# A two-layer hybrid transformer block: ScalarE's gate operations of the context stream put in one fixed order by function table, and the query multiplied by its sigmoid

## The chip, the core and the metric

The kernel runs on one core of a Trainium2 chip. The core has a matrix engine (TensorE, PE in the profile; PEld is its weight load), a vector engine (VectorE, DVE), an engine for functions of one element (ScalarE, ACT), a general engine (GpSimd, POOL), and a queue engine (SyncE, SP) that issues DMA transfers. The engines run side by side; each takes its own instructions strictly in order and waits on semaphores for the others. ScalarE evaluates exponentials, logarithms, sigmoids and the like from a function table, and an instruction ACT_TABLE_LOAD in its stream changes the table.

The metric is the device time of the core in microseconds (us).

## The reference

Two streams run through the block: a latent of 512 tokens and a context of 256 tokens, each of width 1024, in float32. Layer 0 mixes tokens by two gated linear recurrences (group A and group B, 4 heads each, run forward and backward), layer 1 by windowed attention; each is followed by a feed-forward network. The change lies in layer 0, in group A's features:

```python
qa = split_heads(jax.nn.silu(a_q) * A_KEY ** -0.5, A_HEADS)
for d, z in enumerate((a_zf, a_zb)):
    f = lb[d] + (1.0 - lb[d]) * jax.nn.sigmoid(z)
    a_dirs.append((qa, split_heads(1.0 - f), va, split_heads(jnp.log(f))))
...
bc = jnp.cumsum(gc, axis=3)          # within a chunk
q_dec = qc * jnp.exp(bc)
k_inv = kc * jnp.exp(-bc)
```

So for each direction the gate goes through a sigmoid, a logarithm, a running sum and two exponentials, and the query through a SiLU, `x * sigmoid(x)`. Group B's gate is a log-sigmoid, made from an absolute value, an exponential and a logarithm, followed by a running sum and exponentials. A recurrent state passes from chunk to chunk, and from the context's end to the latent's start; the context's recurrence comes first.

## The kernel before

Activations lie with features on the 128 partitions and tokens along the free dimension. Each float32 weight matrix comes in tiles of 128x1024 from memory (`raw`, four buffers) and is split into a high part, rounded by ScalarE (`whi`, L139), and the rest, subtracted by VectorE (`wlo`, L140), three buffers each. Every product is three matmuls: high by high, high by low, low by high. A projection of 128 output features is 24 matmuls (L188; for the value and gate tiles, where the activations are the stationary operand, L198 to L200).

The program is written with generators. `merge(main, side, ratio)` takes one step of `main` and then `ratio` steps of `side` in turn; the order in which instructions are written is their priority, moved forward by `cfg["pri"]` places for weight loads and conversions and by `cfg["evp"]` for the copies that empty PSUM. From that a planner, which simulates the engines, makes each engine's order: at each moment it places the first ready instruction by priority. `follow(key, ins)` adds an order without a wait: an instruction with the same key on the same engine may not be placed ahead of the one before it.

The stage of the change, for the context (`SC`; a tile holds two heads, 128x512):

- `rec_group_a(SC)` runs twelve projections: four for the backward gate (s = 2), four for the query (s = 0), four for the forward gate (s = 1). The gates leave PSUM through a sigmoid on ScalarE (L707), the query through a copy on VectorE (L711). The weights of the first six have `pri` 0, of the others 200. The buffers in PSUM rotate over two named "mm" and three named "kv". Then come the value projections, `rec_v_group(SC, 0)`.
- After that `merge` runs, at ratio 3.2, a main line of twelve steps (`rec_group_b`: the low-rank projection L776, the gate's second matrix L783, four projections of query and key; `rec_v_group`; `rec_group_g`) with a side line: `gla_a(SC)`, `gla_b_feat(SC)`, `norm_lat0()`.
- `gla_a` takes the backward direction first. Its first four steps hold only gate operations: the query's SiLU (L950), the logarithm (L958, after VectorE's scaling L957), and for each of two tiles 1 - f (L962), the running sum (`scan_gate`, L831), a difference (L967), edge values on GpSimd (L822, L823), two exponentials (L969, L970), the query's product (L971) and the key's (L972). `trans_a` (L850) makes one small exponential for the decay from chunk to chunk. Then, for each pair of chunks, the key is transposed on TensorE and copied by ScalarE (`kT`, L858), scores and key-value products are formed, the state goes through a product on GpSimd (`S`, L995) and a sum on VectorE (`R`, L1001), and the output (`ps_o`) is taken (`ob`, L1012 to L1019). The forward direction follows in the same way.
- `gla_b_feat` makes group B's features (absolute value L1039, exponential L1040, logarithm L1043, exponentials L1062 and L1063, small exponential L1081), and `norm_lat0` loads the latent (eight tiles), squares it, adds the squares on GpSimd (L361) and normalizes it.

In this order the planner puts ScalarE's gate operations wherever they are ready. The latent's recurrence later runs the same functions with `SL` (a tile holds one head), where group B's exponentials already have a key of their own, "gkl".

Of the kernel before, what the change touches and what calls it, by code (L numbers as in the profile page):

```python
# [11 lines left out]
F32 = mybir.dt.float32  # L12
# [33 lines left out]
def block_kernel(ctx, tc, plan, xT, cT, vecs, w2, cst, atm, rope, ada, rec_a, rec_v, rec_g, rec_o, qk_w, v_w, wo_w, ff_in, ff_out, out):  # L46
# [639 lines left out]
    class Feat:  # L686
        pass
# [3 lines left out]
    def proj_one(st, idx, u):  # L691
        hi, lo = wload(rec_a[idx], 1024)
        p_ = psg()[:, : st.nt]
        gemm_a(p_, [(hi, lo, KD)], u[0], u[1], st)
        return p_

    def rec_group_a(st, u):
# [3 lines left out]
        for s in (2, 0, 1):  # L701
            for h in range(4):
                p_ = proj_one(st, h * 3 + s, u)
                with tc.high_priority(offset=cfg["evp"]):
                    d_ = ch(f.q if s == 0 else f.z[s - 1], st, h)
                    if s and st.name in 'cl':
                        nc.scalar.activation(d_, p_, AF.Sigmoid)  # L707
                    elif {'c': 'd', 'l': 'a'}[st.name] == "a":
# [4 lines left out]

    def rec_group_a2(nh, lat, order, n1):


        ts = {}
        for st in (SC, SL):
            f = feats[st.name]
            f.q = [ut([P, st.r, st.nt], name="qA") for _ in range(4 // st.r)]  # L720
            f.z = [[ut([P, st.r, st.nt], name="zA") for _ in range(4 // st.r)] for _ in range(2)]
        def prod(st, w, s, h):
            f = feats[st.name]
            u = uc if st is SC else ul
            p_ = psg()[:, : st.nt]
            gemm_a(p_, w, u[0], u[1], st)
            with tc.high_priority(offset=cfg["evp"]):
                d_ = ch(f.q if s == 0 else f.z[s - 1], st, h)
                if st is SL and 1:
                    nc.scalar.copy(d_, p_)  # L730
                else:
                    nc.vector.tensor_copy(d_, p_)
        held = []
        def go(a, b):
            for i in range(a, b):
                s, h = order[i]
                if i == nh:
                    yield from lat
                    for a_ in held:
                        prod(SL, *a_)  # L740
                        yield
                if i < nh:
                    w = [(hi, lo, 4) for hi, lo in whold(rec_a[h * 3 + s])]
                    held.append((w, s, h))
                else:
                    w = [wload(rec_a[h * 3 + s], 1024) + (KD,)]
                prod(SC, w, s, h)
                if i >= nh:
                    prod(SL, w, s, h)
                yield  # L750

        return go(0, n1), go(n1, len(order))
# [1016 lines left out]
```

## Time and profile before

| | |
|---|---|
| Time, median of 3 runs | 1786.58 us (1786.05 to 1788.2) |
| The profiled execution: time, span | 1783.1 us, 1780.7 us |
| TensorE's mean granted clock | 0.986 |
| Busy share: PE, DVE, ACT, POOL | 97%, 58%, 47%, 16% |
| The stage of the change, in the profile | about 43 to 194 us |

The busy share of an engine is an average over stages with different limits. In a view by stretches, each engine's busy time stands against the length of the stretch, with the granted clock of TensorE. In a view by groups, a row has line, engine, operation, output and inputs, the count, the busy time, and the mean length of one in ns. In a view of waits, a row says which instruction waited, for which engine's output and line, and how long. In a view in order of time, the first column is the start and the second the length in us; what stands in brackets is the idle time before, and what ended it.

### The profile page before, as it was taken

What the parts mean: (1) busy time and instruction counts of PE and PEld (TensorE: products, weight loads), DVE (VectorE), ACT (ScalarE), POOL (GpSimd) and SP (SyncE); (2) the same over time, 40 slices, a digit from 0 to 9 for tenths busy, and PEclk for the clock granted to TensorE, in tenths of its full rate; (3) what the DMA queues carried; (4) which work ended last, traced back from release to release, by engine and by line L of the source; (5) the groups of instructions that cost most, each with busy time, mean ns of one, the idle gap of its engine ahead of it and who ended that gap; (6) DMA issues with size and microseconds to landing.
All of it is one profiled execution on the core that took longest, in us unless ns stands there. A gap on an engine that the chain in (4) does not pass through costs nothing.

```text
span 1780.7 us, 27528 instructions
## 1 busy us (share of the span) xinstructions
PE 1723.4 (97%) x10807; PEld 1478.9 (83%) x10807; DVE 1037.3 (58%) x1741; ACT 828.4 (47%) x1403; POOL 279.4 (16%) x316
## 2 busy tenths in 40 slices
PE   7989999999999999999999999999899999999997
PEld 3977778798899989988888888987587998888886
DVE  3768544565877636898533436778755853322335
ACT  3975756445845545532222225434756642222232
POOL 1141201222240013100000001124443200000003
PEclk9989999999999999999999999999999999999998
DMA  8536556211335554767535324341021433233323
GB/s 309 165 121 208 171 189 206 94 58 48 95 120 146 174 158 148 245 225 253 168 110 185 94 76 139 108 120 60 1 60 36 150 114 102 79 100 107 96 68 114
DMA packets 87825, 232.39 MB, mean 131 GB/s; under 512 B 10096, under 2 KB 18032, under 8 KB 87696
## 3 DMA queue, kind: packets, MB, share of 16 engines
q1 hardware_dynamic: 87696, 230.64, 41.0%
q8 instruction: 84, 1.38, 0.3%
q14 instruction: 45, 0.37, 0.1%
HBM read 225.36 MB, written 2.10 MB: 128 GB/s over the span
## 4 chain that ended last, share of the span: by engine, by line
PE 88%; DVE 5%; ACT 4%; issue 2%; DMA 0%; SPq 0%; POOL 0%; DVEq 0%; ACTq 0%
PE ps_mm L188 35%; PE ps_kv L188 31%; PE ps_o L1495 2%; PE ps_o L231 2%; PE ps_tr L1488 2%; PE ps_mm L198 2%; PE ps_mm L199 2%; PE ps_mm L200 2%; PE ps_mm L266 1%; PE ps_kv L266 1%; PE ps_tr L231 1%; PE ps_kv L1454 1%; PE ps_tr L377 1%; PE ps_kv L231 1%; ACT whi L139 1%
## 5 line engine op out<-in xcount | busy, mean ns | idle before, releaser
L139 ACT CAST whi<-raw 128x1024 fp32r<-128x1024 f32 (+3 forms) x304 | 298.2, 982 | 568.5 <-issue 215.6
L140 DVE TENSOR_TENSOR wlo<-raw,whi 128x1024 fp32r<-128x1024 f32 (+3 forms) x314 | 365.9, 1166 | 332.8 <-ACT whi L139 322.7
L188 PE MATMUL ps_mm<-uh,whi 128*128 128x512 f32 (+1 forms) x808 | 277.0, 343 | 2.9 <-ACT whi L139 2.9
L188 PE MATMUL ps_mm<-uh,wlo 128*128 128x512 f32 (+1 forms) x808 | 275.3, 341 | 0.3 <-DVE wlo L140 0.3
L188 PE MATMUL ps_mm<-ul,whi 128*128 128x512 f32 (+1 forms) x808 | 274.7, 340 | 0.0
L188 PE MATMUL ps_kv<-uh,whi 128*128 128x512 f32 (+1 forms) x744 | 260.6, 350 | 0.0
L188 PE MATMUL ps_kv<-uh,wlo 128*128 128x512 f32 (+1 forms) x744 | 259.5, 349 | 0.4 <-DVE wlo L140 0.4
L188 PE MATMUL ps_kv<-ul,whi 128*128 128x512 f32 (+1 forms) x744 | 259.7, 349 | 0.0
L361 POOL TENSOR_TENSOR acc<-acc,sq 128x256 f32<-128x256 f32 (+1 forms) x71 | 88.8, 1253 | 998.3 <-ACT sq L360 993.6
L188 PEld LDWEIGHTS ps_mm<-uh,whi 128*128 128x128 f32 x808 | 154.8, 192 | 22.4 <-ACT whi L139 4.2
L188 PEld LDWEIGHTS ps_mm<-uh,wlo 128*128 128x128 f32 x808 | 154.7, 191 | 17.9 <-issue 0.9
L188 PEld LDWEIGHTS ps_mm<-ul,whi 128*128 128x128 f32 x808 | 154.7, 192 | 16.0 <-issue 0.3
L188 PEld LDWEIGHTS ps_kv<-uh,whi 128*128 128x128 f32 x744 | 140.8, 189 | 21.9 <-ACT whi L139 3.4
L188 PEld LDWEIGHTS ps_kv<-uh,wlo 128*128 128x128 f32 x744 | 140.7, 189 | 18.8 <-DVE wlo L140 0.6
L188 PEld LDWEIGHTS ps_kv<-ul,whi 128*128 128x128 f32 x744 | 140.8, 189 | 18.0 <-issue 0.2
L198 PE MATMUL ps_mm<-whi,uh 128*128 128x256 f32 x344 | 100.1, 293 | 4.0 <-ACT gate L804 4.0
L199 PE MATMUL ps_mm<-wlo,uh 128*128 128x256 f32 x344 | 98.8, 288 | 5.1 <-DVE wlo L140 5.1
L188 PE MATMUL ps_mm<-hh,wlo 128*128 128x256 f32 (+1 forms) x299 | 99.8, 334 | 0.9 <-DVE wlo L140 0.9
L188 PE MATMUL ps_mm<-hh,whi 128*128 128x256 f32 (+1 forms) x299 | 100.0, 334 | 0.0
L188 PE MATMUL ps_mm<-hl,whi 128*128 128x256 f32 (+1 forms) x299 | 99.6, 333 | 0.0
L200 PE MATMUL ps_mm<-whi,ul 128*128 128x256 f32 x344 | 98.7, 288 | 0.0
L298 DVE SCALAR_TENSOR_TENSOR aacc<-ar,s,aacc 128x512 f32<-128x512 f32 x112 | 81.3, 758 | 27.3 <-DMA ar<-in_ada_dram 26.7
(323 smaller groups left out, 3362.1 us busy)
## 6 DMA issues: line engine op xcount, KB each, us to landing
raw<-in_ff_in_dram SPq DMA_DIRECT2D x138, 512.0 KB, 3.6
ar<-in_ada_dram SPq DMA_DIRECT2D x192, 256.0 KB, 4.3
raw<-in_ff_out_dram SPq DMA_DIRECT2D x52, 512.0 KB, 3.6
raw<-in_rec_a_dram SPq DMA_DIRECT2D x34, 512.0 KB, 4.5
raw<-in_rec_v_dram SPq DMA_DIRECT2D x16, 512.0 KB, 3.7
raw<-in_rec_g_dram SPq DMA_DIRECT2D x16, 512.0 KB, 3.7
raw<-in_rec_o_dram SPq DMA_DIRECT2D x16, 512.0 KB, 3.6
raw<-in_wo_w_dram SPq DMA_DIRECT2D x14, 512.0 KB, 3.6
```

What stands on the lines that cost most here:

```text
L139: behind(nc.scalar.copy(hi[:, :n], raw[:, :n]))
L140: behind((nc.gpsimd if cfg["lo"][q % len(cfg["lo"])] == "p" else nc.vector).tensor_sub(lo[:, :n], raw[:, :n], hi[:, :n].bitcast(F32)))
L188: mm(ps_, a, b, start=(i == 0), stop=(i == len(q) - 1))
L198: mm(ps, ah, hi[:, s], start=(k == 0), stop=False)
L199: mm(ps, ah, lo[:, s], start=False, stop=False)
L200: mm(ps, al, hi[:, s], start=False, stop=(k == KD - 1))
L231: yield lambda *a, **k: follow(key, mm(*a, **k))
L266: mm(r[32 * g : 32 * g + 32, :], s32[:, k, 30 - 2 * i : 62 - 2 * i], raw, start=(i == 0 and k < 4), stop=(i == n - 1 and k >= 4), tile_pos ...
L298: nc.vector.scalar_tensor_tensor(a, raw, s_, a, ALU.mult, ALU.add)
L361: (nc.vector if i else nc.gpsimd).tensor_add(d, d, q)
L1488: nc.tensor.transpose(tr[:, g * 128 : (g + 1) * 128], Ps[g][:, j * 128 : (j + 1) * 128], ident)
L1495: mm(o[64 * i : 64 * i + 64, :256], VT[kt][:, kv * 64 : kv * 64 + 64], t_[:, 256 * i : 256 * i + 256], start=(j == 0), stop=(j == len(ktil ...
```

## The change

The gate part of `gla_a` becomes a function of its own, `gate_a(st, d)`, with the query's product in `query_a(st, d)`; the result is kept in `f.a[d]`. For the context both are called while `rec_group_a` is still being written: the backward gate after four projections, the query's sigmoid and product after eight, the forward gate after twelve, ahead of the value projections. For the latent they are called in `gla_a` as before, with the query's products after all of a direction's gate operations, and one more step of the generator for each direction.

`tables(st)` gives the key "tables" for the context and none for the latent. All of the context's sigmoids, logarithms and exponentials of groups A and B, and the SiLU of its output gates, get that key in `follow`, so ScalarE has to take them in the order in which they are written: four sigmoids, two logarithms, five exponentials (backward); two sigmoids of the query; four sigmoids, two logarithms, five exponentials (forward); then group B's two exponentials, two logarithms, seventeen exponentials; then the output gates. The context's query is no longer put through a SiLU but through a sigmoid into a new tile, `qs`, and VectorE multiplies the two. Of the context's weights now the first eight have `pri` 0. An unused variant of the projections (`rec_group_a2`, and the branch on `SH`) is removed.

```diff
+    def tables(st):
+        return "tables" if st is SC else None
+
+    def silu_q(st):
+        f = feats[st.name]
+        if st is SL:
+            for q in f.q:
+                nc.scalar.activation(q, q, AF.Silu)
+        else:
+            for q in f.q:
+                g = ut([P, st.r, st.nt], name="qs")
+                follow(tables(st), nc.scalar.activation(g, q, AF.Sigmoid))
+                nc.vector.tensor_mul(q, q, g)
...
-                    if s and st.name in 'cl':
-                        nc.scalar.activation(d_, p_, AF.Sigmoid)
+                    if s:
+                        follow(tables(st), nc.scalar.activation(d_, p_, AF.Sigmoid))
...
-        nc.scalar.activation(e, e, AF.Exp)
+        follow(tables(st), nc.scalar.activation(e, e, AF.Exp))
...
+    def gate_a(st, d):
+        f = feats[st.name]
+        n = st.nch
+        nt4 = 4 // st.r
+        qd, kd = [], []
+        DL = base.tile([P, 4, n], F32, name=uid("dl"), tag=f"dlA{st.name}", bufs=2)
+        BM = base.tile([P, 4, n], F32, name=uid("bm"), tag=f"bmA{st.name}", bufs=2)
+        g0 = gi[0]
+        for i in range(nt4):
+            s = f.z[d][i]
+            for r in range(st.r):
+                h = d * 4 + i * st.r + r
+                nc.vector.tensor_scalar(s[:, r, :], s[:, r, :], oml[:, h : h + 1], lb[:, h : h + 1], ALU.mult, ALU.add)
+            follow(tables(st), nc.scalar.activation(b65(gpad[(g0 + i) % NG])[:, :, 1:65], v8(s, st), AF.Ln))
+        yield
+        for i in range(nt4):
+            s = f.z[d][i]
+            nc.vector.tensor_scalar(s, s, -1.0, 1.0, ALU.mult, ALU.add)
+            bx = scan_gate()
+            E = ut([P, st.r, st.nt], name="E")
+            Ei = ut([P, st.r, st.nt], name="Ei")
+            i0, i1 = decay(bx, d, ALLP)
+            nc.vector.tensor_sub(v8(Ei, st), i0, i1)
+            edge(bx, d, ALLP, flat8(DL, st, i), flat8(BM, st, i))
+            follow(tables(st), nc.scalar.activation(E, Ei, AF.Exp))
+            follow(tables(st), nc.scalar.activation(Ei, Ei, AF.Exp, scale=-1.0))
+            nc.vector.tensor_mul(Ei, Ei, s)
+            qd.append(E)
+            kd.append(Ei)
+            yield
+        f.a[d] = (qd, kd, DL, trans_a(st, d, DL, BM))
+
+    def query_a(st, d):
+        f = feats[st.name]
+        for E, q in zip(f.a[d][0], f.q):
+            nc.vector.scalar_tensor_tensor(E, E, 128.0 ** -0.5, q, ALU.mult, ALU.mult)
...
         for d in (1, 0):
...
+            if d not in f.a:
+                if d == 1:
+                    silu_q(st)
                 yield
-            e = trans_a(st, d, DL, BM)
+                yield from gate_a(st, d)
+                query_a(st, d)
+                yield
+            qd, kd, DL, e = f.a[d]
...
     def gk(st):
-        return "gk" + st.name if st.name in 'l' else None
+        return "gk" + st.name if st is SL else tables(st)
...
-            nc.scalar.activation(tl[i], tl[i], AF.Exp, scale=-1.0)
+            follow(tables(st), nc.scalar.activation(tl[i], tl[i], AF.Exp, scale=-1.0))
...
-            nc.scalar.activation(tl[i], tl[i], AF.Ln, bias=1.0)
+            follow(tables(st), nc.scalar.activation(tl[i], tl[i], AF.Ln, bias=1.0))
...
-        nc.scalar.activation(e, e, AF.Exp, scale=1.0 / 16.0)
+        follow(tables(st), nc.scalar.activation(e, e, AF.Exp, scale=1.0 / 16.0))
...
-        ga = rec_group_a(SC, uc)
-        for i in range(6):
-            cfg["pri"] = 0 if i < 4 else 0
-            next(ga)
-        cfg["pri"] = 200
-        drain(ga, rec_v_group(SC, 0, uc))
+    ga = rec_group_a(SC, uc)
+
+    def steps(n):
+        for _ in range(n):
+            next(ga)
+
+    steps(4)
+    drain(gate_a(SC, 1))
+    steps(4)
+    silu_q(SC)
+    query_a(SC, 1)
+    cfg["pri"] = 200
+    steps(4)
+    drain(gate_a(SC, 0))
+    query_a(SC, 0)
+    drain(rec_v_group(SC, 0, uc))
```

More of the change, by code (lines that the diff above doesn't have):

```diff
@@ L686, in block_kernel, with __init__ @@
     class Feat:
-        pass
+        def __init__(self):
+            self.a = {}
     feats = {"l": Feat(), "c": Feat()}
@@ L705, in rec_group_a @@
                     d_ = ch(f.q if s == 0 else f.z[s - 1], st, h)
-                    if s and st.name in 'cl':
-                        nc.scalar.activation(d_, p_, AF.Sigmoid)
-                    elif {'c': 'd', 'l': 'a'}[st.name] == "a":
+                    if s:
+                        follow(tables(st), nc.scalar.activation(d_, p_, AF.Sigmoid))
+                    elif st is SL:
                         nc.scalar.copy(d_, p_)
@@ L712, in rec_group_a @@
                 yield
[L714 to L752, printed above, removed]
     def rec_v_group(st, g, u):
@@ L936, in gla_a @@
         npair = n // 2
-        nt4 = 4 // st.r
         is_l = st is SL
@@ L1199, in block_kernel @@
     cfg["pri"] = 0
-    SH = 0
-    zside = iter(())
-    if SH:
-        order = [(s, h) for s in [2, 0, 1] for h in range(4)]
-        n1 = 8
-        ga, rest = rec_group_a2(3, norm_lat0(), order, n1)
-        drain(seq(ga, rec_v_group(SC, 0, uc)))
-    else:
-        rest = iter(())
-        ga = rec_group_a(SC, uc)
-        for i in range(6):
-            cfg["pri"] = 0 if i < 4 else 0
-            next(ga)
-        cfg["pri"] = 200
-        drain(ga, rec_v_group(SC, 0, uc))
+    ga = rec_group_a(SC, uc)
+    def steps(n):
+        for _ in range(n):
+            next(ga)
+    steps(4)
[8 more added lines that the diff above has]
+    drain(rec_v_group(SC, 0, uc))
     rr["tags"] = ["mm"]
@@ L1217, in block_kernel @@
     rr["tags"] = ['mm']
-    drain(merge(seq(rest, rec_group_b(SC, uc), rec_v_group(SC, 1, uc), rec_group_g(SC, uc)), seq(gla_a(SC), gla_b_feat(SC), norm_lat0()), 3.2))
+    drain(merge(seq(rec_group_b(SC, uc), rec_v_group(SC, 1, uc), rec_group_g(SC, uc)), seq(gla_a(SC), gla_b_feat(SC), norm_lat0()), 3.2))
     engines("la")
@@ L1222, in block_kernel @@
     ycs, yoc, yac = new_u(SC), new_ys(SC), Acc(SC)
-    drain(merge(merge(seq(rec_v_group(SL, 0, ul)) if SH else seq(rec_group_a(SL, ul), rec_v_group(SL, 0, ul)), ada_gen(0, (2, 4, 3, 5), ada0), 1.8),
+    drain(merge(merge(seq(rec_group_a(SL, ul), rec_v_group(SL, 0, ul)), ada_gen(0, (2, 4, 3, 5), ada0), 1.8),
                 seq(gla_b(SC), gate_y(SC, 0, ycs), gate_y(SC, 1, ycs), rec_out(SC, ycs, yoc, yac)), 2.0))
```

32 lines of the change are left out of this document (removed).

## Prediction

> **What bounds the kernel now.** I read the page's first part, then a table of stretches of the context's recurrent stage, then what TensorE waited for there, then ScalarE's groups and its instructions in order of time.
>
> ```profile
> span 1780.7 us, 27528 instructions
> PE 1723.4 (97%) x10807; PEld 1478.9 (83%) x10807; DVE 1037.3 (58%) x1741; ACT 828.4 (47%) x1403; POOL 279.4 (16%) x316
> ```
>
> TensorE (PE) is busy 97% of the span, so ScalarE (ACT) at 47% sets the end only in places where PE is idle or slowed. The stage of the change is one of them. Columns of the next view: stretch, length, busy time of PE, PEld, DVE, ACT and POOL with counts, then PE's granted clock, share and rate of the DMA engines.
>
> ```profile
> 43.00:53.00 10.00, 10.00 (x86) 10.00 (x85) 8.19 (x11) 9.66 (x13) 1.83 (x2) 1.00 0.58 180
> 53.00:68.00 15.00, 14.59 (x122) 14.39 (x121) 11.18 (x16) 14.79 (x19) 2.03 (x5) 1.00 0.49 152
> 68.00:88.00 20.00, 18.34 (x153) 18.14 (x153) 15.59 (x21) 18.93 (x25) 3.29 (x5) 1.00 0.50 156
> 88.00:113.00 25.00, 20.03 (x145) 16.71 (x144) 15.04 (x18) 20.27 (x38) 7.00 (x14) 0.83 0.29 100
> ...
> 130.00:143.00 13.00, 9.26 (x77) 8.38 (x78) 11.92 (x15) 5.00 (x8) 7.70 (x6) 0.96 0.44 129
> 143.00:160.00 17.00, 17.00 (x118) 14.93 (x119) 11.57 (x19) 4.95 (x9) 0.00 (x0) 0.83 0.62 194
> ```
>
> From 43 to 88 us ACT is the fullest engine beside PE (43.4 of 45 us), yet PE loses only 0.41 + 1.66 us: the weights are converted ahead. From 88 to 113 PE loses 4.97 us and its clock falls to 0.83. From 130 to 143 it loses 3.74 us, with ACT busy for 5.0 of 13 us. So a lighter ACT can buy time between 68 and 113 us and hardly behind that. The waits of PE from 43 to 165 us (us in total, times, longest) say for whom:
>
> ```profile
> PE ps_mm L199 <- DVE wlo L140: 2.9, 2, 1.7
> PE ps_kv L231 <- ACT kT L858: 2.9, 1, 2.9
> PE ps_o L231 <- POOL S L995: 1.9, 1, 1.9
> PE ps_kv L198 <- ACT whi L139: 1.7, 1, 1.7
> PE ps_o L231 <- ACT ob L1017: 1.5, 1, 1.5
> ```
>
> Three of the five are on ACT, 1.7 + 2.9 + 1.5 us. ACT's own groups from 43 to 113 us show what fills it (count, then busy us and mean ns):
>
> ```profile
> L707 ACT ACT_TABLE_LOAD x4 | 5.1, 1283 | 0.1
> L958 ACT ACT_TABLE_LOAD x4 | 5.1, 1283 | 0.1
> L969 ACT ACT_TABLE_LOAD x2 | 2.6, 1283 | 0.0
> L950 ACT ACT_TABLE_LOAD x2 | 2.6, 1283 | 0.0
> L850 ACT ACT_TABLE_LOAD x2 | 2.6, 1283 | 0.0
> L1043 ACT ACT_TABLE_LOAD x2 | 2.6, 1283 | 0.0
> L1062 ACT ACT_TABLE_LOAD x1 | 1.3, 1283 | 0.0
> L1081 ACT ACT_TABLE_LOAD x1 | 1.3, 1283 | 0.0
> ```
>
> That is 18 loads of a function table, 18 x 1.283 = 23.1 us. The same engine in order of time (start, length):
>
> ```profile
> 66.40 0.63 ACT L950 ACTIVATE qA<-qA 128x512 f32<-128x512 f32 x1
> ...
> 67.99 1.28 ACT L707 ACT_TABLE_LOAD   x1
> 69.28 0.39 ACT L707 ACTIVATE zA<-ps_kv 128x256 f32<-128x256 f32 x1
> ...
> 96.25 0.63 ACT L1043 ACTIVATE lsg<-lsg 128x512 f32<-128x512 f32 x1
> ...
> 98.29 1.28 ACT L1062 ACT_TABLE_LOAD   x1
> 101.37 0.42 ACT L1062 ACTIVATE exB<-aB 64x256 f32<-64x256 f32 x1 [1.80 <-DVE aB L1052]
> ...
> 102.55 0.59 ACT L858 COPY kT<-ps_tr 128x512 f32<-128x512 f32 x1
> ...
> 107.55 0.56 ACT L1017 COPY ob<-ps_o 64x512 f32<-64x512 f32 x1
> ```
>
> A SiLU (L950) followed by a sigmoid (L707) costs a load, and so does a logarithm (L1043) followed by an exponential (L1062): sigmoid, SiLU, logarithm and exponential need four different tables here. The copy of kT that PE waited 2.9 us for stands behind such a load and behind an exponential that itself waits 1.80 us for VectorE (DVE); the copy of ob stands behind the second logarithm. PE's matmuls after that wait:
>
> ```profile
> 104.53 0.40 PE L188 MATMUL ps_mm<-ul,whi 128*128 128x256 f32 x1
> 104.73 0.41 PE L188 MATMUL ps_mm<-uh,wlo 128*128 128x256 f32 x1
> ...
> 114.46 0.41 PE L188 MATMUL ps_mm<-ul,whi 128*128 128x256 f32 x1
> ...
> 115.08 0.28 PE L188 MATMUL ps_mm<-uh,wlo 128*128 128x256 f32 x1
> 115.20 0.28 PE L188 MATMUL ps_mm<-uh,whi 128*128 128x256 f32 x1
> ```
>
> From 104.5 to 114.5 us they start 0.20 to 0.21 us apart, from 115.1 on 0.12 us: a slow spell follows the gap. It is 10.0 us long, less the 1.5 us wait for ob in it 8.5 us of work, of which (0.21 - 0.12) / 0.21 = 43% is lost, 3.7 us.
>
> **The change part by part.** *Table loads.* With the context's operations in one fixed order ACT runs: sigmoids of the backward gate, logarithms, exponentials; sigmoids of the query and of the forward gate, logarithms, exponentials and with them the first exponentials of the second head group; its logarithms; its exponentials. That is 8 loads in place of 18, since the query's sigmoid shares the gate's table, which its SiLU did not. 10 x 1.283 = 12.8 us leave ACT: 8 loads among the gates and the query (14 before, all but those of L1043, L1062 and L1081; 6 after), which lie before 88 us, and 2 in the second group's features (4 before).
>
> What of it reaches the end? Between 43 and 80 us nothing: PE has at most 0.41 us of idle time there. The 1.66 us at 82 us (weights behind the loads of the forward gate) I count in full, since the forward gate's sigmoids, logarithms and exponentials then need 3 loads, where each of its logarithms and sigmoids could take one of its own. For the stall of 88 to 113 us there are 2.9 + 1.5 + 3.7 = 8.1 us to be had at most and nothing at least. Of the four loads of the second group's features (L1043 twice, L1062, L1081) two stay; the exponential's wait for DVE stays as well. I take half, 4.1 us. Sum: 1.7 + 4.1 = 5.8 us gained.
>
> A rule weighed here: by the Trainium skill, "TensorE: Matmul & The Clock Gate", Part 1, PE's clock falls to half for a whole window of some 3.4 us, which runs freely, once PE idles in it. The doubled spacing agrees with the half; the spell's length here is three such windows. By that rule the 3.7 us would be gained whole or not at all, so that the sum would be 1.7 + 2.2 + 3.7 = 7.6 or 3.9 us, about the same middle.
>
> A second one bears on the size: "ScalarE: Activation LUTs", What ACT_TABLE_LOAD costs, gives 2.66 us for a switch with its drain. The rows show 1.29 us from the load's start to the next instruction's (67.99 to 69.28). By the page 26.6 us would leave ACT; the row decides.
>
> *The query.* Two SiLUs of 0.63 us become two sigmoids of the same shape, for which the trace has no row from SBUF; from PSUM a sigmoid of half that width takes 0.39 us, so between 0.6 and 0.8 us, no change. Two multiplications are added on DVE.
>
> ```profile
> L972 DVE TENSOR_TENSOR Ei<-Ei,zA x12: 677/692/1528, 54.8 to 385.9; 128x512 f32<-128x512 f32 x12
> 130.01 5.79 DVE L1065 TENSOR_TENSOR EiB<-exiB,qkB 64x256 f32<-64x256 f32 x4
> 137.57 1.71 DVE L1065 TENSOR_TENSOR EiB<-exiB,qkB 64x256 f32<-64x256 f32 x4
> 129.50 6.02 POOL L361 TENSOR_TENSOR acc<-acc,sq 128x512 f32<-128x512 f32 x4
> ```
>
> By L972 they cost 2 x 0.69 = 1.4 us. They lie at about 63 to 67 us, where PE works from weights converted ahead and DVE is idle 3.8 of 15 us: nothing, or 1.4 us if that cover is gone.
>
> *The moved steps.* The gates issue no transfer. In program order they now pass the conversions, and the transfers on SP's queue, of the weights of projections 5 to 12; the seventh and eighth also lose their head start of 200 places. Cover: four raw and three converted buffers, each worth a projection of 24 matmuls at 0.12 us, 2.9 us. If it were gone, a conversion would stand open, 1.05 us on ACT and 1.23 us on DVE (like the pair at 82 us): 2.3 us for each weight, at most 4.6 us. I take 0, since ACT gets 8 x 1.28 = 10.3 us freer in that same stretch.
>
> *The new order as a wait.* The forward gate's sigmoids empty PSUM, and they now queue behind the backward gate's last exponential, which waits for GpSimd (POOL), and behind the query's sigmoids. PE would notice once all five buffers of "mm" and "kv" were full, 5 x 2.9 = 14 us late, many times the 1.80 us of the wait before an exponential quoted above. Nothing. Square roots are outside the order: one that falls between two exponentials costs two loads, 2.6 us of ACT; between 0 and that, and I take 0 on the path because ACT is idle about 8 of 13 us from 130 us on, where they run.
>
> *The side work.* In the stage's merge the eight side steps that held only gates are gone. At 3.2 side steps to a main step everything behind them is emitted 2.5 main steps earlier: the chain of states, the second group's features, the latent's norm with its eight loads of x on SP (DMA share 0.29 there, room enough) and its adds on POOL. DVE's product group takes 5.79 us beside these adds, 1.71 us after them; PE's 2.9 us of waits for wlo come from such lengthened DVE work. Which operations meet after the change the trace can't tell: between 2.9 us better and 2.9 us worse, taken as 0.
>
> *The latent.* Its table order is unchanged. Its four products E times q for each direction now follow the other products, 4 x 0.69 = 2.8 us later at worst; one more yield per direction shifts the merge a little.
>
> ```profile
> 300.00:400.00 100.00, 99.40 (x720) 83.40 (x719) 59.86 (x95) 50.28 (x82) 23.05 (x32) 0.98 0.25 82
> 400.00:500.00 100.00, 93.84 (x808) 88.05 (x808) 69.94 (x93) 65.68 (x105) 27.05 (x35) 1.00 0.26 80
> ```
>
> PE's projections hide that (99.40 of 100 us). If they did not, it would cost up to 2 x 2.8 us; the 6.2 us idle after 400 us show that the latent's chain can bite. I take 0.
>
> **How the sum stands to the runs.** The profiled execution took 1783.1 us, 2.4 us around its span. 1783.1 - 5.8 = 1777.3 us. The median of the runs is 1786.6, 3.5 us above that execution, so I forecast 1786.6 - 5.8 = 1780.8 us.
>
> **The rivals.** *A: the whole stall goes.* With two loads fewer and the forward gate out of the way the kT and ob copies come in time, no slow spell follows, and DVE's product group no longer meets the adds: 1.7 + 8.1 + 2.9 = 12.7 us, 1773.9 us. For it: the chain through 88 to 113 us is mostly ACT. Against: the exponential's wait for DVE is no table load.
>
> *B: hidden anyway.* The stall moves to the next link of the state chain, and only 1.7 us come back: 1784.9 us. For it: half the waits of the list above are on DVE and POOL. Against: the slow spell begins with an ACT wait.
>
> *C: slower.* The chain of states begins 2.5 main steps earlier and loses the projections that stood between its links. Each link needs PE, ScalarE or DVE, and POOL's product S in turn; already now PE waits 1.9 us for S. One new gap of the size of the kT wait, 2.9 us, with a slow spell of 3.7 us after it, on top of the stall that is there, less 1.7 us: +4.9 us, 1791.5 us. It decides from the point where PE's idle times add up to about 3 us within a few: the 1.7 us at 82 us left the clock at 1.00 (68 to 88 us), the 3.74 us between 130 and 143 us were followed by 0.83. Against: any ready projection can fill in, and the later main steps remain as filler.
>
> *D: it doesn't do what it says.* Square roots or waits split the groups, and the loads stay above 14. Then it ends like B or, with the later products, at 1786.6 us.
>
> **How the numbers follow.** Forecast 0.42 (its own range 1777 to 1783), A 0.20, B 0.16, C 0.18, D 0.04. The low end is A with part of the 3 us that the slow clock costs from 143 to 160 us (17 x 0.17): 1771. The high end is C: 1792. Runs of this kernel differ by about 0.1%, and 0.2% (3.6 us) is what a measurement can tell from no change: faster 0.42 + 0.20 = 0.62, the same 0.16 + 0.04 = 0.20, slower 0.18.
>
> **What would show it.** Right: about 8 loads in ACT's groups from 43 to 113 us; no wait of PE for whi near 82 us; the wait for kT under 1.5 us; a granted clock above 0.83 in the stretch that answers to 88 to 113 us; the later stages shifted by 5 to 6 us as a block. Wrong: PE gaps before 80 us (the order starves the projections); a wait for S, or a slow spell, longer than now; or an equal gain at 194 us that is lost again by 500 us in the latent's chain.

## The result, and the profile after

The changed kernel takes 1769.28 us (median of 4, 1769.22 to 1773.75), the kernel before beside it 1786.32 us (median of 4): a ratio of 0.9914, with a 95% interval of 0.9900 to 0.9929. That is 17.0 us, three times the 5.8 us of the forecast, and 1.7 us below the range.

The profiled execution took 1769.22 us, 13.9 us less than the profiled one of before. The first part of its page:

```profile
span 1766.4 us, 27507 instructions
PE 1719.4 (97%) x10807; PEld 1476.2 (84%) x10807; DVE 1029.1 (58%) x1743; ACT 812.6 (46%) x1391; POOL 276.5 (16%) x316
```

The span lost 14.3 us: PE's idle time fell by 10.3 us (57.3 to 47.0), its busy time by 4.0 us with the same 10807 matmuls, and that is less slow clock. ACT lost 15.8 us of work.

The same stretches of the context's recurrent stage (columns as in the prediction):

```profile
53.00:68.00 15.00, 15.00 (x128) 15.00 (x126) 13.98 (x20) 12.88 (x18) 2.89 (x6) 1.00 0.50 155
68.00:88.00 20.00, 20.00 (x170) 20.00 (x169) 17.52 (x24) 14.43 (x23) 3.65 (x5) 1.00 0.57 182
88.00:113.00 25.00, 19.86 (x146) 16.59 (x146) 12.74 (x17) 20.45 (x41) 9.13 (x15) 0.87 0.33 109
...
130.00:143.00 13.00, 11.56 (x100) 10.60 (x99) 9.80 (x14) 5.76 (x9) 7.11 (x5) 1.00 0.61 198
```

From 53 to 88 us PE has no idle time left, and ACT has some. From 88 to 113 us almost nothing moved: PE idles 5.14 us (4.97 before), the clock is 0.87 (0.83). Behind 113 us, where the prediction expected hardly anything, PE idles less: 1.44 us from 130 to 143 us, 3.74 before. The waits of PE from 43 to 165 us:

```profile
PE ps_o L231 <- POOL S L982: 3.3, 2, 1.9
PE ps_kv L231 <- DVE R L988: 2.7, 1, 2.7
PE ps_mm L757 <- ACT lr L752: 0.5, 1, 0.5
PE ps_kv L266 <- DMA ar<-in_ada_dram: 0.5, 1, 0.5
```

The waits for kT, ob, whi and wlo are all gone. In their place stand waits for the state chain, on S (3.3 us, 1.9 before) and on R (2.7 us, new). ACT's groups from 43 to 113 us, its table loads and the query's sigmoid:

```profile
L923 ACT ACT_TABLE_LOAD x2 | 2.6, 1283 | 0.0
L934 ACT ACT_TABLE_LOAD x2 | 2.6, 1283 | 0.0
...
L723 ACT ACT_TABLE_LOAD x1 | 1.3, 1283 | 0.0
L710 ACT ACT_TABLE_LOAD x1 | 1.3, 1283 | 0.0
L1030 ACT ACT_TABLE_LOAD x1 | 1.3, 1283 | 0.0
L1049 ACT ACT_TABLE_LOAD x1 | 1.3, 1283 | 0.0
```

Eight loads in place of 18, as predicted. Two rows in order of time, the first latent sigmoid of before and of after, show how much of the gain is there when the context hands over to the latent:

```profile
196.25 0.60 ACT L707 ACTIVATE zA<-ps_mm 128x512 f32<-128x512 f32 x1
```

```profile
189.04 0.60 ACT L723 ACTIVATE zA<-ps_mm 128x512 f32<-128x512 f32 x1
```

7.2 us are there; another 7.1 us come later, so the later stages did not shift as one block. The latent's stretch and that of the windowed attention, after, and the attention's, before:

```profile
400.00:500.00 100.00, 95.93 (x820) 90.54 (x820) 70.67 (x91) 64.12 (x104) 25.92 (x36) 1.00 0.31 92
...
1130.70:1359.30 228.60, 220.96 (x1510) 177.06 (x1511) 163.93 (x463) 123.79 (x295) 87.20 (x101) 0.97 0.20 59
```

```profile
1139.80:1373.50 233.70, 222.29 (x1512) 178.56 (x1514) 167.16 (x463) 125.00 (x296) 86.29 (x101) 0.97 0.20 58
```

From 400 to 500 us PE idles 2.1 us less than before (93.84 to 95.93). The attention, where the change edits nothing, is 5.1 us shorter, 3.8 us of it less idle time. The planner's order there is another one all the same: compared place by place, the two traces have another matmul at 113 of PE's places between 1100 and 1300 us. 7.2 + 2.1 + 5.1 = 14.4 us is the whole difference of the two spans.

### The profile page after: what moved, and what is told of

It reads as the page before. It is cut to its first block, busy times and chain, and to the rows that moved or that the text cites. A ratio compares the mean times of both kernels' runs of the same rounds, so it can differ in the third digit from the quotient of the medians.

```text
span 1766.4 us, 27507 instructions
## 1 busy us (share of the span) xinstructions
PE 1719.4 (97%) x10807; PEld 1476.2 (84%) x10807; DVE 1029.1 (58%) x1743; ACT 812.6 (46%) x1391; POOL 276.5 (16%) x316
## 4 chain that ended last, share of the span: by engine, by line
PE 91%; DVE 5%; ACT 2%; issue 1%; DMA 1%; POOL 0%; SPq 0%; DVEq 0%; ACTq 0%; POOLq 0%
PE ps_mm L188 37%; PE ps_kv L188 32%; PE ps_tr L1476 2%; PE ps_o L1483 2%; PE ps_o L231 2%; PE ps_mm L198 2%; PE ps_mm L199 2%; PE ps_mm L200 2%; PE ps_kv L266 1%; PE ps_tr L231 1%; PE ps_mm L266 1%; PE ps_kv L231 1%; PE ps_tr L377 1%; PE ps_kv L1442 1%; PE ps_kv L1443 1%
## 5 line engine op out<-in xcount | busy, mean ns | idle before, releaser
L188 PEld LDWEIGHTS ps_mm<-uh,wlo 128*128 128x128 f32 x808 | 154.8, 192 | 17.6 <-issue 0.7
L188 PEld LDWEIGHTS ps_mm<-ul,whi 128*128 128x128 f32 x808 | 154.8, 192 | 15.8
```

Of the source, the lines that this page charges most:

```text
L188: mm(ps_, a, b, start=(i == 0), stop=(i == len(q) - 1))
```

## The experiments

Two theories stood at the start. The one called T1: the gain has a share of the context (its fewer loads) and a share of the latent's moved products. T2: the latent's part does nothing, the context's change is all. When the first runs had split the change by place, a second question came up: are the ten loads the cause, or the order that removes them, or the early place of the gates? Each run was timed beside the kernel before, whose median in these sets was 1786.5 to 1786.7 us. Ratios are to it, with 95% intervals. The views come from one profiled execution of each run; where that one lies far from the median, its time is given.

**ctx_only.** The change for the context alone; the latent's query products stay where they were.

```diff
+            if st is SL:
+                nc.vector.scalar_tensor_tensor(E, E, 128.0 ** -0.5, f.q[i], ALU.mult, ALU.mult)
...
                 yield from gate_a(st, d)
-                query_a(st, d)
-                yield
```

> The change for the context alone; the latent's gate part is written as before (query's product between the exponentials and the key's product, no extra step). Theory 1 (two causes: 7 us in the context's stage through the order by table; the other 7 us from another order that the planner finds for the latent and the attention, set off by the latent's moved products): the latent's first sigmoid comes about 7 us earlier than before (near 189 us), and the end about 7 us earlier plus whatever its own order in the attention gives, 1774 to 1781 us. Theory 2 (one cause: all of it follows from the context being done earlier): the whole gain, 1769 to 1772 us.

Measured: 1778.67 us (1774.82 to 1783.35), 0.9960 (0.9946 to 0.9974), eight loads. The time is T1's, but the first latent sigmoid is at 195.7 us in the profiled execution, the slowest of the eight (1783.35 us), where 189 was expected: from 130 to 143 us the clock is 0.75 there and PE idles for 2.5 us (1.00 and 1.44 us in the changed kernel).

**lat_only.** The kernel before, with the latent's query products moved behind the other products and one more yield.

```diff
-                nc.vector.scalar_tensor_tensor(E, E, 128.0 ** -0.5, f.q[i], ALU.mult, ALU.mult)
+                if not is_l:
+                    nc.vector.scalar_tensor_tensor(E, E, 128.0 ** -0.5, f.q[i], ALU.mult, ALU.mult)
...
             e = trans_a(st, d, DL, BM)
+            if is_l:
+                for E, q in zip(qd, f.q):
+                    nc.vector.scalar_tensor_tensor(E, E, 128.0 ** -0.5, q, ALU.mult, ALU.mult)
+                yield
```

> The kernel before, with the latent's query products behind all of a direction's gate operations and one more step of the generator for each direction, as in the change; the context as before. From the latent's recurrence on, the planner gives TensorE the same order as in the changed kernel. Theory 1: the latent's first sigmoid at about 196 us as before, but the end 5 to 8 us earlier than before, 1778 to 1782 us. Theory 2: no change, 1784 to 1788 us.

Measured: 1782.94 us (1773.87 to 1785.92, 12 executions), 0.9976 (0.9960 to 0.9992): a gain of 4.3 us by the ratio (3.6 us in the medians), where T2 had nothing, so T2 falls, though the interval ends close to 1. It is 0.9 us outside T1's range. The profiled execution, at 1774.12 us, is one of the three fastest of the twelve. Its stretch of the latent:

```profile
400.00:500.00 100.00, 95.92 (x822) 90.00 (x821) 70.62 (x91) 63.60 (x102) 24.64 (x36) 1.00 0.28 85
```

The same 95.92 us as in the changed kernel: the 2.1 us of idle time between 400 and 500 us go with the moved products.

**no_order.** The changed kernel without the order by table: early gates and the query's sigmoid remain.

```diff
-        return "tables" if st is SC else None
+        return None
```

> The change without its fixed order: the gates are written at their new, earlier places and the query is multiplied by its sigmoid, but nothing orders ScalarE's functions by table. From the latent's recurrence on the planner's order is that of the changed kernel. If the 7 us of the context's stage come from the fewer table loads: loads between 43 and 113 us back above 13, and the latent's first sigmoid at 194 to 197 us, the time at 1776 to 1780 us. If they come from the earlier place of the gates (eight empty side steps gone, more work written earlier): loads many, yet the sigmoid near 189 us and the time near 1770 us.

Measured: 1784.99 us (1775.22 to 1787.51, 12), 0.9991 (0.9977 to 1.0006): no difference from before. In the profiled execution (1775.22 us, the fastest of the twelve) the first latent sigmoid is at 198.78 us. The largest waits of PE from 43 to 165 us:

```profile
PE ps_mm L198 <- ACT qkB L767: 3.8, 1, 3.8
PE ps_kv L231 <- ACT kT L834: 2.2, 1, 2.2
PE ps_o L231 <- POOL S L982: 1.5, 1, 1.5
PE ps_o L231 <- ACT ob L1004: 1.3, 1, 1.3
```

17 loads are back, and the waits for ACT with them. The early place and the sigmoid alone give nothing; the fixed order is what works. The time is higher than was expected of it, so the latent's 4.3 us of lat_only do not show here either.

**order_only.** The kernel before, with the order by table and the query's sigmoid; the gates stay at their old place, the latent as before.

```diff
+    def tables(st):
+        return "tables" if st is SC else None
...
-                for i in range(nt4):
-                    nc.scalar.activation(f.q[i], f.q[i], AF.Silu)
+                for q in f.q:
...
+                        g = ut([P, st.r, st.nt], name="qs")
+                        follow(tables(st), nc.scalar.activation(g, q, AF.Sigmoid))
+                        nc.vector.tensor_mul(q, q, g)
...
-                nc.scalar.activation(E, Ei, AF.Exp)
+                follow(tables(st), nc.scalar.activation(E, Ei, AF.Exp))
```

> The kernel before, its gates written where they were, after the projections and inside the merge, with only the order by table and the query's sigmoid added: all sigmoids of gates and query, then logarithms and exponentials of each direction. The latent as before. Loads from 43 to 113 us fall to 6 to 8. If fewer loads are the cause: the latent's first sigmoid at 189 to 191 us. If the place is the cause: at 195 to 197 us, or later, since the backward logarithms now wait for the forward sigmoids, about 20 us more.

Measured: 1766.66 us (1762.77 to 1769.85, 5), 0.9894 (0.9875 to 0.9912), with seven loads: all of the gain, without moving a gate. The first latent sigmoid is at 179.87 us, 9 us earlier than was expected of fewer loads. PE's waits from 43 to 165 us, and then two stretches:

```profile
PE ps_mm L785 <- ACT lr L780: 1.1, 1, 1.1
...
PE ps_o L231 <- POOL S L1004: 0.2, 1, 0.2
```

```profile
88.00:113.00 25.00, 23.87 (x165) 20.64 (x164) 22.09 (x30) 21.48 (x41) 11.68 (x18) 0.80 0.34 108
113.00:160.00 47.00, 46.13 (x395) 41.29 (x394) 38.91 (x55) 29.86 (x53) 16.69 (x14) 1.00 0.62 203
```

Hardly any wait remains. That the gates, as steps of the side line, keep the links of the state chain apart may be the reason; no run shows it, and empty steps in their place (padded, below) don't do it. A slow spell (0.80) is there all the same.

**after_again.** The changed kernel once more, unedited, so that it is timed on the same chip as the others.

> The changed kernel once more, for a distribution of its time beside that of the kernel before on one chip: executions of one kernel lie up to 12 us apart with the granted clock (0.983 to 0.990 in one of the runs above). If the gain of 15 to 17 us is a property of the kernel: median 1768 to 1772 us. If its first four executions were lucky in their slow spells: median 1773 to 1778 us, clocks from 0.984 to 0.988.

Measured: 1770.08 us (1767.57 to 1773.86, 6), 0.9909 (0.9890 to 0.9927). With the first four executions the median of ten is 1769.28 us.

**loads_back.** The changed kernel with five tiny sigmoids (128x1, on a tile that nothing reads) put into the fixed order, each of which forces two loads. Every engine's order is otherwise that of the changed kernel.

```diff
+    def other(st, fn):
+        if st is SC:
+            follow(tables(st), nc.scalar.activation(tiny, ones, fn))
...
             follow(tables(st), nc.scalar.activation(b65(gpad[(g0 + i) % NG])[:, :, 1:65], v8(s, st), AF.Ln))
+            if i == 0:
+                other(st, AF.Sigmoid)
...
             follow(tables(st), nc.scalar.activation(Ei, Ei, AF.Exp, scale=-1.0))
+            if i == 0:
+                other(st, AF.Sigmoid)
...
             follow(tables(st), nc.scalar.activation(tl[i], tl[i], AF.Exp, scale=-1.0))
+            if i == 0:
+                other(st, AF.Sigmoid)
```

> The changed kernel with five sigmoids of one column (0.2 us each) put into the fixed order between the two logarithms, between the exponentials of the first and the second tile, and between group B's first two exponentials: 18 table loads from 43 to 113 us as before the change, and every engine's order of all other instructions exactly that of the changed kernel. If the loads' own time on ScalarE is what the change took off the path: the waits for kT, ob or whi come back, the latent's first sigmoid at 193 to 197 us, the median 5 to 16 us above the changed kernel's. If the new order of the work did it, and the loads lie in ScalarE's idle time: the sigmoid at 189 to 191 us, the median within 3 us of the changed kernel's.

Measured: 1782.61 us (1777.5 to 1785.6, 12), 0.9977 (0.9962 to 0.9991), 13.3 us above the changed kernel. In turn: what was put on ACT (groups), and what PE then waits for beside the R and S of the changed kernel (the largest two):

```profile
L706 ACT ACT_TABLE_LOAD x5 | 6.4, 1283 | 0.1
L706 ACT ACTIVATE tiny<-ones 128x1 f32<-128x1 f32 x5 | 1.0, 204 | 0.1
```

```profile
PE ps_mm L763 <- ACT lr L758: 2.1, 1, 2.1
PE ps_mm L188 <- ACT whi L139: 1.4, 1, 1.4
```

The order of all other instructions is the same in the two traces, matmul by matmul, so each can be set beside itself. In order of time: PE's wait for R in the changed kernel, the same wait here, and the first latent sigmoid here:

```profile
104.64 0.93 PE L231 MATMUL ps_kv<-v,kT 64*128 64x128 f32 x10 [2.71 <-DVE R L988]
```

```profile
115.45 0.93 PE L231 MATMUL ps_kv<-v,kT 64*128 64x128 f32 x10 [2.46 <-DVE R L998]
```

```profile
200.18 0.60 ACT L729 ACTIVATE zA<-ps_mm 128x512 f32<-128x512 f32 x1
```

Ten loads and five tiny operations are 10 x 1.283 + 1.0 = 13.8 us of ACT. The matmul behind R is 10.8 us late, the latent's sigmoid 200.18 - 189.04 = 11.1 us: nearly all of the delay arises up to this matmul, while the loads run, and almost nothing is added behind. The waits for kT and ob don't come back, that for whi does, and the sigmoid is 3 us later than either expectation had it. The attention makes up some 2 us of it, so that the profiled execution (1777.5 us, the fastest of the twelve) ends 8.3 us behind the profiled one of the changed kernel; in the medians it is 13.3 us. Resampling the executions of the two kernels gives 8 to 15 us as a 95% interval. So ten loads together cost most of their length in this order; the main finding rests on this run.

**padded.** The changed kernel with four empty steps put back before each direction of the context, so that the chain of states starts where it did.

```diff
+            if st is SC:
+                for _ in range(4):
+                    yield
             qd, kd, DL, e = f.a[d]
```

> The changed kernel with four empty steps put back in front of each direction of the context's recurrence, so that the merge writes the chain of states, the second group and the latent's norm beside the same main steps as before. Table order and places of the gates as in the change. If the earlier side work is what leaves TensorE's waits for R and S in the changed kernel (6.0 us between 43 and 165 us): these fall below 2.5 us, the latent's first sigmoid comes before 186 us, the median 3 to 8 us below the changed kernel's. If not: waits and time as in the changed kernel.

Measured: 1772.9 us (1770.98 to 1775.7, 6), 0.9925 (0.9909 to 0.9941), not faster than the changed kernel, and its first two waits are unchanged:

```profile
PE ps_o L231 <- POOL S L985: 3.3, 2, 1.9
PE ps_kv L231 <- DVE R L991: 2.7, 1, 2.7
```

For the waits and the time the expectation failed: the eight side steps that went are not what makes S and R late. One of its signs came, though: the first latent sigmoid is at 184.10 us, 4.9 us earlier than in the changed kernel. From 320 to 345 us this execution has a clock of 0.73, where the changed kernel's has 1.00, and the lead is gone by 400 us.

**order_lat.** order_only with the latent's part of the change (the diff of lat_only).

> The order by table with the gates at their old place (the fastest of the runs so far, 1766.7 us), and with it the latent's part of the change (query products last, one more step). If the latent's part is worth what its own run showed (3.6 us in the median): 1762 to 1765 us. If that difference came from slow spells of the clock: 1765 to 1769 us.

Measured: 1770.16 us (1765.04 to 1773.69, 6), 0.9906 (0.9886 to 0.9926). That is above both expected ranges: the latent's part gives nothing there, and the intervals of the two overlap.

**loads_early** and **loads_late.** loads_back in two halves: four loads in the backward gate alone (ahead of 65 us), and the other six.

```diff
-            if i == 0:
+            if i == 0 and d == 1:
                 other(st, AF.Sigmoid)
```

> The changed kernel with 4 of the 10 loads put back, all in the backward gate (before about 64 us): one tiny sigmoid between its logarithms, one between the exponentials of its two tiles; every engine's order otherwise that of the changed kernel. The prediction held that loads before 80 us cost the end nothing, since TensorE has converted weights in hand there: then the median is that of the changed kernel, 1768 to 1772 us, and TensorE has no wait before 80 us. If each load delays what is queued behind it on ScalarE, all the way to the end, 4 loads and two tiny sigmoids cost about 5.5 us: 1773 to 1777 us.

> The changed kernel with the other 6 loads put back: 4 in the forward gate (about 76 to 88 us) and 2 between group B's first exponentials (about 95 us); order otherwise that of the changed kernel. If only the loads from 80 us on count: the whole 12.5 us that the ten loads cost together, 1780 to 1784 us. If all loads count alike: 6 loads and three tiny sigmoids, about 8 us, 1776 to 1780 us.

Measured: loads_early 1777.64 us (1776.42 to 1781.36, 6), 0.9959 (0.9942 to 0.9975), 8.4 us above the changed kernel for 5.5 us of ACT; loads_late 1778.46 us (1776.31 to 1783.39, 9), 0.9963 (0.9951 to 0.9976), 9.2 us for 8.3 us of ACT. Both cost, the early ones no less. The order of all other instructions is again that of the changed kernel. Of loads_early: PE's waits from 43 to 90 us and the first stretch; then, in order of time, a load that was put back, the conversion of a weight behind it, and PE's wait for that; last the same conversion in the changed kernel:

```profile
PE ps_mm L188 <- ACT whi L139: 1.4, 1, 1.4
PE ps_mm L188 <- DVE wlo L140: 0.8, 1, 0.8
```

```profile
43.00:88.00 45.00, 42.78 (x340) 42.12 (x339) 34.40 (x47) 38.13 (x52) 5.15 (x11) 0.96 0.50 155
```

```profile
60.40 1.28 ACT L706 ACT_TABLE_LOAD   x1
...
67.39 1.03 ACT L139 CAST whi<-raw 128x1024 fp32r<-128x1024 f32 x1
```

```profile
68.47 0.39 PE L188 MATMUL ps_mm<-uh,whi 128*128 128x256 f32 x1 [1.42 <-ACT whi L139]
```

```profile
63.83 1.04 ACT L139 CAST whi<-raw 128x1024 fp32r<-128x1024 f32 x1
```

The early loads delay this conversion by 3.6 us, PE waits 1.4 us for it and 0.8 us for the rest, and the clock of the stretch is 0.96 where it was 1.00. At the first latent sigmoid loads_early is 3.2 us behind the changed kernel (192.19 us), loads_late 3.0 us (192.02); after_again, unedited, is 0.7 us ahead (188.34). So each half costs 3 to 4 us there, of 5.5 and 8.3 us of ACT, and the two together less than the 11.1 us of all ten: the costs don't simply add.

The rest of the 8.4 and 9.2 us isn't lost where the loads are. Both profiled executions lose 6.2 us between 320 and 345 us, where nothing was edited. The stretch in the changed kernel, in after_again and in loads_early:

```profile
320.00:345.00 25.00, 24.40 (x129) 18.04 (x128) 14.38 (x33) 10.64 (x16) 5.24 (x5) 1.00 0.17 52
```

```profile
320.00:345.00 25.00, 24.40 (x91) 16.84 (x90) 13.25 (x33) 9.47 (x15) 5.24 (x5) 0.73 0.08 23
```

```profile
320.00:345.00 25.00, 24.41 (x90) 16.80 (x89) 12.82 (x33) 8.99 (x14) 6.26 (x6) 0.73 0.20 63
```

It is a slow spell that one execution of the changed kernel has and another hasn't. Whether a delay of 3 us brings it on or chance does is open; no execution of the two runs is below 1776.3 us.

**both_logs.** order_only with the logarithms of both directions together, which saves two more loads (five).

```diff
-            for i in range(nt4):
-                s = f.z[d][i]
+            for d_, i in [(d, i) for i in range(nt4)] if is_l else [(e_, i) for e_ in (1, 0) for i in range(nt4)] if d else []:
+                s = f.z[d_][i]
```

> The order by table at the old place, with the logarithms of both directions written together ahead of the first exponential: 5 loads in place of 7. If each load is worth about 1.25 us at the end, as ten of them were (12.5 us): 2 to 3 us below the kernel with 7, near 1764 us. If the loads that are left are hidden, or the backward exponentials lose by waiting for two more logarithms (1.2 us): the same as that kernel, 1766 to 1769 us, or above.

Measured: 1770.92 us (1769.54 to 1772.69, 5), 0.9918 (0.9902 to 0.9934): not faster than with seven loads, 4.1 us above the median of that kernel's ten executions (order_again, below). The backward exponentials now stand behind the forward gate's logarithms, so the backward chain starts later; that this eats the 2.6 us wasn't separated.

**order_again.** order_only once more, unedited.

> The order by table at the old place (7 loads, latent as before) once more beside the kernel with 5 loads and on the same chip; it took 1766.7 us in five executions that lay 7 us apart. If it beats the changed kernel by itself: median 1764 to 1768 us; if its five executions were lucky: 1769 to 1773 us.

Measured: 1766.9 us (1763.85 to 1770.5, 5), 0.9895 (0.9876 to 0.9913). The median of its ten executions is 1766.8 us, 2.5 us below that of the changed kernel's ten, with ranges that overlap. So the version that writes the order down and moves nothing is at least as fast as the change.

## Why the prediction was wrong, and where it was right

The direction was right, and so was the cause that it named: the fixed order takes ten loads off ScalarE, and with the ten put back most of the gain is gone. The step that failed is the one that says where the time comes back: "a lighter ACT can buy time between 68 and 113 us and hardly behind that". The sum has 5.8 us there and nothing elsewhere; the side work, the new order and the latent stand in it at 0. In the profiles the stretches from 43 to 113 us gave 2.7 us of 14.3: 2.1 us before 88 us, where 1.7 us were counted, and 0.6 us in the stall, where 4.1 us were. Some 6.7 us came between 113 and 160 us. These are estimates from idle time and clock; the execution of after starts the stage 1.0 us later, and at the hand-over to the latent 7.2 us are there. Another 7.1 us came behind it.

A count of matmuls says where, without a choice of stretches. The table has the times, in us, at which PE starts its 500th, 640th, 1010th, 1880th and 2600th matmul, worked out from the traces (in after these are at about 88, 113, 160, 300 and 400 us), and the span. Where the order differs, the matmuls up to a number aren't all the same ones; in after, after_again and the three runs with loads put back they are.

| | loads, 43 to 113 us | 500th | 640th | 1010th | 1880th | 2600th | span |
|---|---|---|---|---|---|---|---|
| before | 18 | 89.8 | 115.3 | 167.1 | 307.4 | 407.4 | 1780.7 |
| no_order | 17 | 90.7 | 114.8 | 167.3 | 308.6 | 409.1 | 1773.4 |
| ctx_only | 8 | 87.7 | 111.9 | 163.5 | 304.5 | 409.5 | 1780.7 |
| after | 8 | 88.2 | 112.4 | 159.1 | 299.4 | 399.8 | 1766.4 |
| after_again | 8 | 87.4 | 111.7 | 158.4 | 298.7 | 406.9 | 1772.0 |
| loads_early | 12 | 92.0 | 115.6 | 162.3 | 302.6 | 408.7 | 1775.5 |
| loads_late | 14 | 88.2 | 115.4 | 162.1 | 302.4 | 408.6 | 1775.4 |
| loads_back | 18 | 93.0 | 123.2 | 170.3 | 310.5 | 411.0 | 1774.9 |
| order_only | 7 | 87.5 | 109.9 | 154.8 | 292.1 | 396.9 | 1764.9 |

From the 640th to the 1010th matmul before takes 51.8 us and after 46.7. The loads' own time isn't the reason: in after's order it is 46.7 to 47.1 us with 8, 12, 14 or 18 loads, and 52.5 us in no_order, where the gates are early but nothing is ordered. So the gain behind 113 us hangs on the order that the planner makes of the work. The key alone doesn't bring it: ctx_only, which has the key, takes 51.6 us there, with a clock of 0.75 from 130 to 143 us. The price of the loads lies ahead of it: by the 640th matmul loads_back is 10.8 us behind after, about twice the forecast for the whole, and 7.9 us behind before, which has as many loads. What a load costs thus hangs on the order. In the old one, where the planner put each operation wherever it was ready, 18 loads cost less than in the new one. In the new one even "Between 43 and 80 us nothing" fails, by the 3 us of loads_early: PE waits there for a conversion that stands behind the loads. Why the work between 113 and 160 us is shorter in after's order no run has taken apart.

Point by point:

- *Table loads, 18 to 8:* right, count and length. The query's sigmoids too: 0.63 us each (626 ns in the group's row below), inside 0.6 to 0.8 us.

```profile
L710 ACT ACTIVATE qs<-qA 128x512 f32<-128x512 f32 x2 | 1.3, 626 | 0.0
```

- *The wait at 82 us, 1.7 us in full:* right. It is gone, and 53 to 88 us gained 2.1 us (14.59 + 18.34 to 35.00).
- *The stall of 88 to 113 us, 4.1 us:* wrong, too high. The kT and ob waits went as predicted, but R and S took their place: idle time 4.97 to 5.14 us. With the clock 0.83 to 0.87 the slow share falls from 20.03 x 0.17 = 3.4 to 19.86 x 0.13 = 2.6 us; some 0.6 us net. The slow spell after the gap stayed, but shorter: in the traces' record of the clock it lasts from 106.6 to 113.4 us, where it lasted from 104.5 to 114.8, two windows of 3.4 us in place of three. By the rule weighed in the prediction (the Trainium skill, "TensorE: Matmul & The Clock Gate", Part 1) it was to go whole or not at all; here a third of it went. The condition that the Trainium skill gives there is an idle window; in the window before the spell PE idles for 2.1 us in before and 2.5 us in after, so here part of one was enough.
- *Behind 113 us, 0:* wrong, and this made up for it. The view by stretches from 113 to 160 us, of before and of after:

```profile
113.00:160.00 47.00, 42.17 (x322) 38.14 (x322) 36.53 (x47) 22.32 (x40) 16.12 (x13) 0.91 0.52 163
```

```profile
113.00:160.00 47.00, 45.07 (x374) 39.05 (x373) 38.86 (x54) 23.38 (x39) 15.13 (x12) 1.00 0.57 188
```

  2.9 us less idle time, and 42.17 x 0.09 = 3.8 us of slow clock gone: 6.7 us. The range of -2.9 to 2.9 us for the side work named the place rightly, but held only the idle time; the slow clock that goes with it was left out of the bound and appeared only at the low end of the whole range. VectorE's products beside GpSimd's adds are in it. One of the two product groups, the row of the groups from 43 to 165 us in before, in after, and (the third) in ctx_only:

```profile
L1064 DVE TENSOR_TENSOR EB<-exB,qkB 64x256 f32<-64x256 f32 x8 | 7.2, 901 | 0.1
```

```profile
L1051 DVE TENSOR_TENSOR EB<-exB,qkB 64x256 f32<-64x256 f32 x8 | 4.1, 509 | 0.1
```

```profile
L1051 DVE TENSOR_TENSOR EB<-exB,qkB 64x256 f32<-64x256 f32 x8 | 8.2, 1022 | 0.1
```

  It got faster in after and slower in ctx_only, with the same eight loads: which operations meet is indeed a matter of the order, and the prediction had said that the trace couldn't tell which would.
- *The moved steps, at nothing, and the new order as a wait, at nothing:* right as far as a cost goes. PE has no idle time from 53 to 88 us, and no_order gives no difference from before. That the order could gain time by itself wasn't weighed.
- *The latent, 0:* too low in place, 2.1 us of idle time went between 400 and 500 us in lat_only and after alike. What it is worth at the end stays open (below).
- *Rival A (1773.9 us)* was the nearest, for another reason: it took the stall of 88 to 113 us for the source. *B* (1784.9 us) falls outside every execution. *C*'s waits came, S 1.9 to 3.3 us and R 2.7 us, without its price; padded shows that its reason, the early chain, isn't their cause. Its point of about 3 us of idle time doesn't hold either: the slow spell of after_again at 327 us follows 0.60 us of it. *D* is excluded by the eight loads.

One way from before to after leads over loads_back: the new order with all 18 loads gives 4.1 us in the medians (5.8 us in the profiled spans), taking ten loads out of it 13.3 us (8.5 us). The sum, 17.4 us (14.3 us), is the gain. It is not the only way: what ten loads are worth in the old order no run shows. The first term is about lat_only's 4.3 us, but that it is the latent's part was not shown: the latent's part gave 4.3 us on the kernel before, some 9 us on ctx_only (1778.67 to 1769.28) and nothing on order_only.

By the Trainium skill, "ScalarE: Activation LUTs", What ACT_TABLE_LOAD costs, a switch with its drain is 2.66 us, 26.6 us for ten. Its 1.283 us for the load alone is the row's; of the drain the traces show nothing (0.01 to 0.02 us between a load and its neighbours, where ACT waits for no other engine), and ten loads cost 8.3 to 13.3 us.

Still open: why moving the gates costs 12 us without the latent's part (order_only 1766.8, ctx_only 1778.67) and nothing with it (order_lat 1770.16, changed 1769.28), though by the 1880th matmul order_only is 7.3 us ahead of the changed kernel too; why five loads are no better than seven; and what shortened the attention. There every other trace is 2 to 6 us shorter than that of before (from the 7151st to the 7915th matmul), whichever part of the change it has, and of before there is one trace. PE's two largest waits there, of before, and what answers to them in after, where none for pT is above 0.2 us:

```profile
PE ps_tr L1488 <- DVE pT L1491: 3.9, 2, 3.1
PE ps_kv L1454 <- DVE mx L1457: 3.6, 4, 2.4
```

```profile
PE ps_o L1483 <- DVE Ol L1490: 2.5, 1, 2.5
PE ps_kv L1442 <- DVE mx L1445: 1.7, 4, 0.6
```

## What to carry to other kernels

Where one engine feeds the bottleneck in strict order, a busy bottleneck is no proof that work put on the feeder is hidden: four loads put where TensorE had shown no wait cost 3 us at the hand-over, since a conversion stood behind them. Nor has a load one price: here it hung on the order around it. Test a price by putting the removed cost back with every order otherwise kept, as loads_back does; undoing the change also changes what meets what. Then compare each instruction with itself: a stretch of fixed times holds other work once the traces are shifted. Look for slow spells far from the edit before a difference of medians is put down to it. And try the smallest form first: here writing the order down gave the whole gain, and moving the gates earlier gave nothing more.

## What the runs showed of the hardware that was not expected

Executions of one kernel differ by more than the three runs of before let expect, and the differences go with the granted clock. The twelve of lat_only fall into two groups, three near 1774 us at a mean clock of 0.990 and nine near 1783 us at 0.983. Over 55 executions of before the mean clock is 0.9835, over the ten of the changed kernel 0.9868: (1 - clock) x span is 29.4 and 23.3 us, so some 6 of the 17 us go with the slow clock. Two executions of the changed kernel, the profiled one and that of after_again, differ by 6.2 us between 320 and 345 us, in the latent's projections (rows under loads_early).

PE is equally busy, 24.40 us of 25, but at a clock of 0.73 it runs 91 matmuls where it ran 129. Both have the same idle time of 0.60 us at about 324 us; behind it the clock is at half from 326.8 to 340.5 us in the one and at full in the other. So a slow clock costs time without a new idle gap, in some executions of a kernel and not in others, and a term for it belongs in the sum beside the waits.
